# Two layers on one core: between the layers, weight splits are held back while the first token tile is normalised, and half of that tile's scaling moves from ScalarE to VectorE

## The chip, the cores and the metric

The kernel runs on one core of one Trainium2 chip. The metric is the device time of one execution in microseconds, and the lower the better. The kernel before was timed three times on the chip; a fourth execution was recorded by the hardware profiler, and all rows below are from that one.

## What is computed

Two transformer blocks of different kinds follow each other on 256 tokens of width 1024, in f32. What matters here is the passage from the first to the second:

```
# end of the first block
    return x + merged @ w_out[l]
...
    return _rmsnorm(x, final_norm_g)
...
# start of the second block
        h = rmsnorm(x, norm1_g[l]) * (1.0 + scale1) + shift1
        proj = h @ w_in[l]
        qa, ka, va, fa, qb, kb, vb, ga, gb = jnp.split(proj, IN_SPLITS, axis=-1)
```

So the output projection `merged @ w_out` and the residual are followed by two RMS norms in a row, a scale and a shift per column (they come from `c_2` through `ada_w_2`), and the input projection of the second block. After that block's attentions comes a mixture of 16 experts, whose weights are about 100 MB, and a last norm.

## The kernel before, in words

**Split matmuls.** A product of f32 matrices is made of three fast products: each operand is split into a high part (rounded to `fp32r`) and a low part (the rest), and low*high, high*low and high*high are summed in PSUM. Activations stand transposed in `H` (high) and `L` (low), eight blocks of 128 columns by 256 tokens. A weight unit is 1024 columns of a 128-row tile; it is split by one ScalarE copy (`self.sc.activation(h, raw, AF.Copy)` in `splitter`) and one VectorE subtraction (`split_low`), both 128x1024 between the layers. In the rows the tiles of split weights are called `w`, those of raw weights `ring`.

**Two token tiles.** The 256 tokens are two tiles of 128, `t` = 0 and 1 (first and second tile below). `out_proj` does `w_out` in eight parts for the first tile, then eight for the second. A part is one weight unit against one tile: six matmuls 128x512, two groups of three. The input projections that follow (`va` and `vb`, four weight units each, written by `job_a`) are woven by `weave` with `LAG2` = 5: five parts of the first tile, and then one of the first and one of the second in turn.

**The norm between the layers**, `mid_norm(t, banks)`, is a generator. On VectorE it adds the two PSUM banks to the residual (`X<-X,d`) and multiplies by a row (`tt<-X,ra`), for each half of the columns; ScalarE makes four sums of squares; VectorE adds them (`v<-ss`) and goes on with small steps; ScalarE takes a root (`s<-v`); five more small steps on VectorE, and then the scaled tile `xs<-tt,r` (128x1024). `affine_split` follows: TensorE transposes `xs` in two halves of four 128x128 blocks (`w<-cf,xs`), each half is multiplied by a column scale and a shift is added (`PP<-w`, four instructions), ScalarE rounds it (`H<-PP`), VectorE subtracts (`L<-PP,H`). Of the first tile both halves are scaled on ScalarE, of the second tile the first half on ScalarE and the second half on VectorE.

**What sets the order.** Instructions are written in the order that `Order`, a model of the engines' times inside the kernel's program, gives: generators are stepped when the modelled time reaches them. Every engine then works its own list in that order. `splitter` is one such generator; it splits the next weight unit as soon as its raw tile is there and a slot for the split tile is free, ahead of need. `self.v.` and `self.sc.` calls all show as L275, matmuls as L436, transposes as L452.

Of the kernel before, what the change touches and what calls it, by code (L numbers as in the profile page):

```python
# [97 lines left out]
class Pack:  # L98


    def __init__(self, x, ap):
        self.x, self.ap = x, ap
        self.parts = []
        self.where = {}
        self.at = 0
# [186 lines left out]
def wait(cond):  # L292
    while not cond():
        yield 0.1
# [27 lines left out]
class Body:  # L322
    def __init__(self, ctx, tc, a, pack):
        self.tc = tc
        self.pk = pack
        self.nc = nc = tc.nc
        self.a = a
        self.o = o = Order()
        self.v = Timed(o, "dve", nc.vector)
        self.sc = Timed(o, "act", nc.scalar)  # L330
        self.fix = ctx.enter_context(tc.tile_pool(name="fix", bufs=1))
        self.big = ctx.enter_context(tc.tile_pool(name="big", bufs=1))
        dram = ctx.enter_context(tc.tile_pool(name="dram", bufs=1, space=bass.MemoryType.DRAM))
        self.xd = dram.tile([2 * P, D], F32, name="xd")
        self.ps = ctx.enter_context(tc.tile_pool(name="ps", bufs=1, space=bass.MemoryType.PSUM))
        self.free = [f"ring{i}" for i in range(5)]
        self.slots = [f"spl{i}" for i in range(4)]
        self.until_unit = {}
        self.at = 0
        self.last_split = False  # L340
        self.pool = {k: [f"{k}{i}" for i in range(n)] for k, n in dict(d=4, w=4, p=4, th=3, sp=3).items()}
        self.held = {}
        self.turn = {}
        self.ada_first = Task(None)
        self.quiet = False
        self.t0_scaled = False
        self.chunks = []
        self.units = []
        self.items = []
        self.live = 0  # L350
        self.act_set = None
        self.exp_set = SET_EXP

# [140 lines left out]
    def splitter(self):  # L494

        for u in self.units:
            self.slots = [x for x in self.slots if self.until_unit.get(x, u.idx) >= u.idx]
            yield from wait(lambda: self.slots)
            u.tag = self.slots.pop(0)
            for c, view, lo, n, shape in u.srcs:  # L500
                while c.tile is None:
                    yield 0.1
                d = self.o.written(c.tile) - self.o.now
                if u.tile is None:
                    d = max(d, self.o.slot_end(u.tag) - self.o.now)
                if d > 0:
                    yield d
                if self.relaxed(u):
                    yield from self.yielding("act")
                if u.tile is None:  # L510
                    u.tile = self.slab(u.tag, "w")
                    u.h = u.tile[:, 0:1024].bitcast(F32R)
                    u.l = u.tile[:, 1024:2048].bitcast(F32R)
                raw = view(c.tile)
                h = u.h[:, lo:lo + n]
                l = u.l[:, lo:lo + n]
                if shape:
                    h = h.rearrange(shape[0], **shape[1])
                    l = l.rearrange(shape[0], **shape[1])
                self.sc.activation(h, raw, AF.Copy)  # L520
                self.o.spawn(self.split_low(u, c, raw, h, l), self.o.next - self.o.now)
                yield max(0.01, self.o.free["act"] - self.o.now - 0.3)
        self.last_split = True
        self.spare(self.slots)
        self.slots = []
# [257 lines left out]
    def affine_split(self, x, t, scale, marks, bias=None):  # L783

        def sink(k0, ps):
            eb = yield from self.take("p")
            e = eb.rearrange("p (j q) -> p j q", j=4)
            for j in range(4):
                k = k0 + j
                q = ps[:, j * P:(j + 1) * P]  # L790
                if (k0 == 0 or t == 0) and bias is not None:
                    self.act(e[:, j], q, AF.Identity, scale=scale[:, k:k + 1], bias=bias[:, k:k + 1])
                elif k0 == 0:
                    self.act(e[:, j], q, AF.Copy, scale=scale[:, k:k + 1])
                elif bias is not None:
                    self.v.tensor_scalar(e[:, j], q, scale[:, k:k + 1], bias[:, k:k + 1], OP.mult, OP.add)
                else:
                    self.v.tensor_scalar(e[:, j], q, scale[:, k:k + 1], None, OP.mult)
            if k0:
                yield  # L800
            h = self.xh[:, k0:k0 + 4, t * P:(t + 1) * P]
            self.act(h, e, AF.Copy)
            yield
            self.v.tensor_tensor(self.xl[:, k0:k0 + 4, t * P:(t + 1) * P], e, h.bitcast(F32), OP.subtract)
            self.drop(eb)
            yield
            marks[k0 // 4].fin = self.o.now
            marks[k0 // 4].done = True

        return self.transposed(x, sink)  # L810
# [384 lines left out]
    def mid_norm(self, t, banks):  # L1195

        v = self.v
        x = self.x[:, t]  # L1200
        ss = self.tmp("ss4", 2, 4)
        cs = [slice(b * 512, (b + 1) * 512) for b in range(2)]
        for b, c in enumerate(cs):
            if t == 1:
                yield from self.yielding("dve")
            v.tensor_tensor(x[:, c], x[:, c], banks[b], OP.add)
            self.drop(banks[b])
            v.tensor_tensor(self.tt[:, t, c], x[:, c], self.row_a[:, c], OP.mult)
        yield 0.7 if t == 0 else None
        for b, c in enumerate(cs):  # L1210
            self.act(self.xs[:, t, c], x[:, c], AF.Square, accum_out=ss[:, b:b + 1])
            self.act(self.xs[:, t, c], self.tt[:, t, c], AF.Square, accum_out=ss[:, 2 + b:3 + b])
        yield
        m = self.tmp("v2", 2, 2)
        s = self.tmp("s2", 2, 2)
        r = self.tmp("r2", 2, 4)
        v.tensor_tensor(m, ss[:, 0:4:2], ss[:, 1:4:2], OP.add)
        v.tensor_scalar(m[:, 0:1], m[:, 0:1], 1.0 / D, EPS, OP.mult, OP.add)
        v.tensor_scalar(s[:, 0:1], m[:, 0:1], EPS, None, OP.mult)
        v.tensor_scalar(m[:, 1:2], m[:, 1:2], 1.0 / D, s[:, 0:1], OP.mult, OP.add)  # L1220
        yield
        yield from self.root(r[:, 0:2], m, s)
        v.tensor_scalar(self.xs[:, t], self.tt[:, t], r[:, 1:2], None, OP.mult)
        yield

        yield from self.affine_split(self.xs[:, t], t, self.a1, self.n_marks[t], self.modc[:, 0])
        self.act(x, self.tt[:, t], AF.Copy, scale=r[:, 0:1])
# [949 lines left out]
```

## Time and profile before

| | |
|---|---|
| median of 3 runs | 714.19 us |
| lowest, highest | 713.5, 714.22 us |
| the profiled execution: time, span of its instructions | 714.5 us, 712.6 us |
| TensorE: busy time, share of the span | 688.1 us, 97% |
| VectorE, ScalarE: share of the span | 56%, 45% |
| DMA: mean rate over the span | 290 GB/s |
| mean granted TensorE clock | 0.984 |

The time of an execution is about 1.9 us longer than the span from its first to its last instruction. A time in a timeline row is counted from the span's start. In a timeline row "x8" is eight like instructions in a row, the second number is how long they took together, and what stands in brackets is how long the engine was idle before, and what it waited for.

### The profile page before, as it was taken

To read this page: it belongs to the slowest core of one execution; us is meant where nothing else is said; L and a number is where in the kernel's file an instruction comes from. 1 tells how busy PE (TensorE), PEld (TensorE's weight loads), DVE (VectorE), ACT (ScalarE), POOL (GpSimd) and SP (SyncE) were. 2 spreads that over 40 slices of the span, in tenths; PEclk is the share of its full clock that TensorE was granted. 3 is DMA by queue.
4 is the path that set the end of the run, shared out by engine and by line. 5 is a ranking of instruction groups with operands and counts; after the bars stand their busy time and mean duration, and the time that the engine had idled before them with its cause. 6 is when DMAs were issued, how large, how long until landed. Compare 5 with 4: busy or idle time off the path is not lost.

```text
span 712.6 us, 9923 instructions
## 1 busy us (share of the span) xinstructions
PE 688.1 (97%) x3860; PEld 492.9 (69%) x3862; DVE 397.5 (56%) x752; ACT 320.0 (45%) x613; POOL 9.1 (1%) x15
## 2 busy tenths in 40 slices
PE   7999999999999998999999999989999999999993
PEld 6999889878878886899877778876333433443431
DVE  6576687896756676686967846653211311321315
ACT  6544475564444667545668744522221121121113
POOL 0000000000000000000000000000000000000000
PEclk8999999999999999999999999999999999999997
DMA  9965657546756553555673895996999999999991
GB/s 354 381 231 220 267 186 282 184 177 236 288 184 245 181 224 119 214 229 204 241 295 137 329 361 183 351 385 268 417 422 420 420 423 420 420 421 418 421 364 63
DMA packets 31668, 206.35 MB, mean 290 GB/s; under 512 B 3968, under 2 KB 4480, under 8 KB 8448
## 3 DMA queue, kind: packets, MB, share of 16 engines
q1 hardware_dynamic: 29968, 200.82, 72.2%
q0 software_dynamic: 1072, 3.68, 1.3%
q10 hardware_dynamic: 576, 1.16, 0.4%
q8 instruction: 32, 0.52, 0.3%
q14 instruction: 20, 0.16, 0.1%
HBM read 203.55 MB, written 2.10 MB: 289 GB/s over the span
## 4 chain that ended last, share of the span: by engine, by line
PE 72%; DMA 21%; DVE 4%; ACT 1%; issue 1%; SPq 0%; DVEq 0%; ACTq 0%
PE d L436 53%; PE w L436 17%; DMA spl<-weights 6%; DMA L<-weights 6%; DMA YA<-weights 6%; DMA ring<-weights 3%; PE w L452 2%; DVE w L275 1%; DMA X<-x 1%; ACT xs L275 0%; DVE PP L275 0%; DVE L L275 0%; DVE X L1597 0%; ACT sq L275 0%; DVE sw L275 0%
## 5 line engine op out<-in xcount | busy, mean ns | idle before, releaser
L275 DVE TENSOR_TENSOR w<-ring,w 128x1024 fp32r<-128x1024 f32 (+1 forms) x166 | 156.6, 964 | 80.0 <-ACT w L275 79.7
L275 ACT ACTIVATE w<-ring 128x1024 fp32r<-128x1024 f32 (+1 forms) x166 | 136.1, 849 | 88.4 <-PE d L436 82.0
L436 PE MATMUL d<-w,H 128*128 128x512 f32 x448 | 141.1, 397 | 0.0
L436 PE MATMUL d<-H,w 128*128 128x256 f32 x672 | 121.8, 283 | 0.0
L436 PEld LDWEIGHTS d<-H,w 128*128 128x128 f32 x672 | 104.7, 192 | 0.1
L436 PEld LDWEIGHTS d<-w,H 128*128 128x128 f32 x448 | 85.9, 192 | 18.0 <-issue 0.5
L436 PE MATMUL d<-L,w 128*128 128x256 f32 x336 | 97.2, 289 | 0.0
L436 PE MATMUL d<-w,L 128*128 128x512 f32 x224 | 93.3, 416 | 3.8 <-DVE L L275 3.8
L436 PEld LDWEIGHTS d<-L,w 128*128 128x128 f32 x336 | 64.4, 192 | 1.2 <-issue 1.0
L1625 DVE TENSOR_TENSOR th<-th,w 128x512 f32<-128x512 f32 (+1 forms) x9 | 5.6, 628 | 102.2 <-PE w L436 102.2
L436 PE MATMUL d<-w,YA 128*128 128x512 f32 x224 | 60.6, 394 | 0.0
L275 ACT ACTIVATE th<-w 128x512 f32<-128x512 f32 (+1 forms) x16 | 9.3, 584 | 106.6 <-PE w L436 53.7
L436 PEld LDWEIGHTS d<-w,L 128*128 128x128 f32 x224 | 43.1, 192 | 14.7 <-DVE L L275 5.2
L275 DVE SCALAR_TENSOR_TENSOR acc<-ring,ca,acc 128x1024 f32<-128x1024 f32 x39 | 49.9, 1280 | 2.3 <-DMA ring<-weights 2.1
L436 PEld LDWEIGHTS d<-w,YA 128*128 128x128 f32 x224 | 41.9, 188 | 9.0 <-issue 0.3
L436 PE MATMUL w<-ring,ra 128*64 128x512 f32 x128 | 47.0, 598 | 0.0
L275 ACT ACTIVATE rg<-th 128x512 fp32r<-128x512 f32 x15 | 9.4, 630 | 55.0 <-DVE th L1652 34.8
L436 PE MATMUL w<-spl,ra 128*64 128x512 f32 x96 | 32.5, 596 | 0.0
L436 PEld LDWEIGHTS w<-ring,ra 128*64 128x64 f32 x128 | 13.5, 137 | 18.2 <-issue 17.7
L436 PE MATMUL w<-ring,th 128*64 128x512 f32 x72 | 25.5, 599 | 0.0
L275 ACT ACTIVATE PP<-w,sa 128x128 f32<-128x128 f32 (+1 forms) x48 | 19.7, 426 | 9.0 <-DVE sa L275 7.5
L436 PE MATMUL d<-w,YC 128*128 128x512 f32 x96 | 23.5, 399 | 0.0
(326 smaller groups left out, 1021.8 us busy)
## 6 DMA issues: line engine op xcount, KB each, us to landing
ring<-weights SPq DMA_DIRECT2D x109, 1024.0 KB, 6.4
spl<-weights SPq DMA_DIRECT2D x16, 1024.0 KB, 18.2
CQ<-weights SPq DMA_DIRECT2D x8, 1024.0 KB, 7.0
AB<-weights SPq DMA_DIRECT2D x6, 1024.0 KB, 14.3
K<-weights SPq DMA_DIRECT2D x6, 1024.0 KB, 13.5
PT<-weights SPq DMA_DIRECT2D x5, 1024.0 KB, 16.2
H<-weights SPq DMA_DIRECT2D x5, 1024.0 KB, 19.2
L<-weights SPq DMA_DIRECT2D x5, 1024.0 KB, 19.8
```

What stands on the lines that cost most here:

```text
L275: r = fn(*args, **kw)
L436: self.nc.tensor.matmul(out, lhsT, rhs, start=start, stop=stop)
L452: self.nc.tensor.transpose(out, in_, self.ident if ident is None else ident)
L1625: nc.vector.tensor_tensor(h[:, c], gate[:, c], res[1][:, c], OP.mult)
```

## The change

Three edits. First, a counter `budget` is put into `splitter`: None lets it split freely, 0 stops it, a positive number is counted down by one for each piece. `mid_norm` sets it to 0 when the first tile's norm begins and to 2 when the tile has been scaled (`xs`); `affine_split` sets it to 1 when the first half of the first tile has been split into `H` and `L`, and to None at the second half. Second, the first tile's second half is scaled on VectorE, as the second tile's is. Third, and by itself, the order in which `Order` steps everything around this place comes out anew.

```diff
@@ splitter
                 if self.relaxed(u):
                     yield from self.yielding("act")
+                yield from wait(lambda: self.budget != 0)
+                if self.budget:
+                    self.budget -= 1
                 if u.tile is None:
                     u.tile = self.slab(u.tag, "w")
...
@@ affine_split
-                if (k0 == 0 or t == 0) and bias is not None:
+                if k0 == 0 and bias is not None:
                     self.act(e[:, j], q, AF.Identity, scale=scale[:, k:k + 1], bias=bias[:, k:k + 1])
...
             self.drop(eb)
+            if bias is not None and t == 0:
+                self.budget = None if k0 else 1
             yield
...
@@ mid_norm
         x = self.x[:, t]
+        if t == 0:
+            self.budget = 0
         ss = self.tmp("ss4", 2, 4)
...
         v.tensor_scalar(self.xs[:, t], self.tt[:, t], r[:, 1:2], None, OP.mult)
+        if t == 0:
+            self.budget = 2
         yield
```

The lists of the engines differ only here, between the layers; before and behind it they read alike, and the DMA queues' lists are alike from end to end.

**VectorE, from the first tile's scaling to the second tile's sums.** Before, from `xs_2398<-tt,r_2433` of the first tile to `v_2551<-ss_2516` of the second (the other tiles are named above):

```order
L275 TENSOR_SCALAR xs_2398<-tt,r_2433 128x1024
L275 TENSOR_TENSOR w<-ring_2288,w 128x1024 x2
L275 TENSOR_TENSOR w<-ring_2328,w 128x1024 x2
L275 TENSOR_TENSOR L<-PP,H 128x4x128
L275 TENSOR_TENSOR X<-X,d_2400 128x512
L275 TENSOR_TENSOR tt<-X,ra 128x512
L275 TENSOR_TENSOR X<-X,d_2401 128x512
L275 TENSOR_TENSOR tt<-X,ra 128x512
L275 TENSOR_TENSOR w<-ring_2364,w 128x1024
L275 TENSOR_TENSOR L<-PP,H 128x4x128
L275 TENSOR_TENSOR v_2551<-ss_2516 128x2
```

Of the change, the same stretch:

```order
L275 TENSOR_SCALAR xs_2398<-tt,r_2431 128x1024
L275 TENSOR_TENSOR w<-ring_2245,w 128x1024 x2
L275 TENSOR_SCALAR PP<-w_2474,a_1548,modc 128x128 x4
L275 TENSOR_TENSOR L<-PP,H 128x4x128 x2
L275 TENSOR_TENSOR X<-X,d_2400 128x512
L275 TENSOR_TENSOR tt<-X,ra 128x512
L275 TENSOR_TENSOR w<-ring_2288,w 128x1024 x2
L275 TENSOR_TENSOR w<-ring_2328,w 128x1024 x2
L275 TENSOR_TENSOR w<-ring_2364,w 128x1024
L275 TENSOR_TENSOR X<-X,d_2401 128x512
L275 TENSOR_TENSOR tt<-X,ra 128x512
L275 TENSOR_TENSOR v_2572<-ss_2504 128x2
```

The pair of `ring_2245`, which stood ahead of the first tile's root, is now behind its scaling; the first tile's two `L` have moved ahead of four of the splits; and five splits now stand between the two halves of the second tile's residual (`d_2400` and `d_2401`), where none stood.

**TensorE, around the second tile's transposes.** Before (`w_2474` and `w_2485` are the two units of one raw tile of `vb`, `d3` is the first tile's sum, `w_2423` the first unit of `va`, and `d0_2608` the second tile's first sum):

```order
L436 MATMUL d3_2572<-w_2474,L_2397 128x512
L436 MATMUL d3_2572<-w_2474,H_2396 128x512 x2
L452 MATMUL w0_2580<-cf_72,xs2_2398 128x128 x4
L452 MATMUL w1_2585<-cf_72,xs2_2398 128x128 x4
L436 MATMUL d3_2572<-w_2485,L_2397 128x512
L436 MATMUL d3_2572<-w_2485,H_2396 128x512 x2
L436 MATMUL d3_2572<-w_2485,L_2397 128x512
L436 MATMUL d3_2572<-w_2485,H_2396 128x512 x2
L436 MATMUL d0_2608<-w_2423,L_2397 128x512
```

Of the change (`w_2528` and `w_2536` are those two units of `vb`, `w_2449` is the first of `va`):

```order
L437 MATMUL d3_2552<-w_2528,L_2397 128x512
L437 MATMUL d3_2552<-w_2528,H_2396 128x512 x2
L437 MATMUL d3_2552<-w_2536,L_2397 128x512
L437 MATMUL d3_2552<-w_2536,H_2396 128x512 x2
L437 MATMUL d3_2552<-w_2536,L_2397 128x512
L437 MATMUL d3_2552<-w_2536,H_2396 128x512 x2
L453 MATMUL w0_2586<-cf_72,xs2_2398 128x128 x4
L453 MATMUL w1_2591<-cf_72,xs2_2398 128x128 x4
L437 MATMUL d0_2608<-w_2449,L_2397 128x512
```

The transposes stand one part later: behind six of the first tile's parts instead of five, and the second tile's first matmul, which reads what comes of them, follows them at once.

**TensorE, around the first tile's transposes.** Before (`w_2361` and `w_2385` are the last two units of `w_out`, here against the second tile; `d2_2520` is the first sum of the second layer):

```order
L436 MATMUL d1_2401<-w_2361,YA_2073 128x512
L452 MATMUL w3_2488<-cf_72,xs2_2398 128x128 x4
L452 MATMUL w2_2496<-cf_72,xs2_2398 128x128 x4
L436 MATMUL d0_2400<-w_2385,CV_2074 128x512
L436 MATMUL d1_2401<-w_2385,CV_2074 128x512
```

Of the change:

```order
L437 MATMUL d1_2401<-w_2352,YA_2073 128x512
L453 MATMUL w3_2466<-cf_72,xs2_2398 128x128 x4
L453 MATMUL w2_2474<-cf_72,xs2_2398 128x128 x4
L437 MATMUL d0_2400<-w_2361,CV_2074 128x512
L437 MATMUL d1_2401<-w_2361,CV_2074 128x512
```

Here the transposes stand one part earlier: two parts of `w_out` are behind them instead of one.

## Rows read from the trace of the kernel before

**Rows 1.** The page: the span, and busy time of each engine.

```profile
span 712.6 us, 9923 instructions
PE 688.1 (97%) x3860; PEld 492.9 (69%) x3862; DVE 397.5 (56%) x752; ACT 320.0 (45%) x613; POOL 9.1 (1%) x15
```

**Rows 2.** Waits of TensorE by what ended them: total us, times, longest.

```profile
PE d L436 <- DVE L L275: 3.8, 3, 1.8
```

**Rows 3.** Timeline of TensorE between the layers: start, us.

```profile
263.63 0.62 PE L436 MATMUL d<-w,CV 128*128 128x512 f32 x2
...
265.00 1.03 PE L452 MATMUL w<-cf,xs 128*128 128x128 f32 x8
...
269.24 0.50 PE L436 MATMUL d<-w,L 128*128 128x512 f32 x1 [1.83 <-DVE L L275]
...
273.68 0.43 PE L436 MATMUL d<-w,L 128*128 128x512 f32 x1
...
277.86 1.04 PE L452 MATMUL w<-cf,xs 128*128 128x128 f32 x8
...
281.44 0.51 PE L436 MATMUL d<-w,L 128*128 128x512 f32 x1 [1.16 <-DVE L L275]
```

**Rows 4.** Windows: length, busy us by engine; PEclk, DMA share, GB/s.

```profile
10.00:14.00 4.00, 2.76 (x10) 2.27 (x11) 4.00 (x11) 3.94 (x12) 0.00 (x0) 0.55 1.02 412
268.00:272.00 4.00, 2.76 (x8) 2.20 (x9) 3.93 (x7) 3.97 (x11) 0.00 (x0) 0.72 0.96 395
...
280.00:284.00 4.00, 2.84 (x13) 2.14 (x12) 1.59 (x3) 3.05 (x4) 0.00 (x0) 1.00 0.00 0
```

**Rows 5.** Timeline of VectorE between the layers.

```profile
256.77 0.68 DVE L275 TENSOR_TENSOR X<-X,d 128x512 f32<-128x512 f32 x1
...
259.07 0.16 DVE L275 TENSOR_TENSOR v<-ss 128x2 f32<-128x2 f32 x1 [0.89 <-ACT xs L275]
...
260.02 2.36 DVE L275 TENSOR_TENSOR w<-ring,w 128x1024 fp32r<-128x1024 f32 x2 [0.16 <-ACT w L275]
...
263.29 0.75 DVE L275 TENSOR_SCALAR xs<-tt,r 128x1024 f32<-128x1024 f32 x1
263.95 4.63 DVE L275 TENSOR_TENSOR w<-ring,w 128x1024 fp32r<-128x1024 f32 x4
...
270.42 0.68 DVE L275 TENSOR_TENSOR X<-X,d 128x512 f32<-128x512 f32 x1
...
271.74 1.22 DVE L275 TENSOR_TENSOR w<-ring,w 128x1024 fp32r<-128x1024 f32 x1
...
273.48 0.15 DVE L275 TENSOR_TENSOR v<-ss 128x2 f32<-128x2 f32 x1
...
275.55 0.76 DVE L275 TENSOR_SCALAR xs<-tt,r 128x1024 f32<-128x1024 f32 x1
278.93 1.37 DVE L275 TENSOR_SCALAR PP<-w,a,modc 128x128 f32<-128x128 f32 x4 [2.63 <-PE w L452]
280.69 1.29 DVE L275 TENSOR_TENSOR L<-PP,H 128x512 fp32r<-128x512 f32 x2 [0.39 <-ACT H L275]
```

**Rows 6.** Timeline of ScalarE between the layers.

```profile
260.94 3.95 ACT L275 ACTIVATE w<-ring 128x1024 fp32r<-128x1024 f32 x4
...
278.50 1.50 ACT L275 ACTIVATE PP<-w,modc,a 128x128 f32<-128x128 f32 x4 [1.21 <-PE w L452]
280.03 1.15 ACT L275 ACTIVATE H<-PP 128x512 fp32r<-128x512 f32 x2
```

**Rows 7.** Timeline of TensorE at the kernel's start: the first block's transposes.

```profile
10.44 1.97 PE L452 MATMUL w<-cf,xs 128*128 128x128 f32 x8 [0.96 <-DVE xs L275]
```

**Rows 8.** Windows of the second layer, its end, and the experts (columns as in Rows 4).

```profile
300.00:472.00 172.00, 171.84 (x1049) 144.21 (x1049) 116.21 (x184) 97.67 (x181) 0.78 (x1) 1.00 0.70 264
488.00:492.00 4.00, 3.94 (x20) 1.23 (x18) 3.37 (x22) 1.39 (x2) 0.00 (x0) 1.00 0.02 6
500.00:530.00 30.00, 29.12 (x140) 10.53 (x136) 5.78 (x15) 6.30 (x11) 0.98 (x1) 1.00 1.01 420
```

More of the change, by code (lines that the diff above doesn't have):

```diff
@@ L350, in __init__ @@
         self.live = 0
+        self.budget = None
         self.act_set = None
```

## The prediction

> **What bounds the kernel now.** I read the page's busy times first: TensorE is busy for 688.1 us of a span of 712.6 [rows 1], so what can be won or lost in the middle is idle TensorE, or TensorE at its lower clock. The list of its waits comes next: matmuls that waited for `L` of VectorE lost 3.8 us in three places [rows 2]. One lies in the first block's beginning; the timeline of TensorE shows the other two, and both are between the layers [rows 3]: 1.83 us at 269.24, where the first tile's first input projection waits for the normalised tile, and 1.16 us at 281.44, where the second tile's does. The first has a sequel. The granted clock over 268 to 272 is 0.72, a mixture of full speed and half (the levels are 2.4 and 1.2 GHz), while behind the shorter second stall it stays at 1.00 [rows 4]. The four groups from 269.24 to 273.68 are two parts [rows 3]; a part at full clock is the 1.37 us from the matmul at 263.63 to the transposes at 265.00, so 4.44 us were spent on 2.74 us of work, 1.70 us lost. All that this place has to give is therefore 1.83 + 1.16 + 1.70 = 4.7 us.
>
> A delay or a gain here reaches the end. From 300 to 472 TensorE is busy for 171.84 of 172 us, so nothing in the second layer takes it up. At 488 to 492 the DMA share is 0.02: the transfers have filled every buffer and wait for TensorE to free one; from 500 on they run at a share of 1.01 [rows 8]. The experts' stream thus starts when TensorE gets there, and is moved with it.
>
> **The first tile, step by step.** *The root earlier.* The pair of splits that filled VectorE from 260.02 for 2.36 us, while the root was wanted, is moved behind the scaling. The second tile of before shows the way from the sums to the scaling with no split between: 273.48 to 275.55, 2.07 us [rows 5]. From 259.07 that gives 261.14 for the scaling and, with its 0.75 us, 261.9 for its end, where before it ended at 264.04. The counter costs no instruction.
>
> *Transposes.* They stand one part earlier, so at 263.63 instead of 265.00 [rows 3], with `xs` ready for 1.7 us by then.
>
> *Half of the scaling on VectorE.* Four take 1.37 us there and 1.50 on ScalarE, and the halves go side by side [rows 5, 6]. The second tile of before is made just so: from its transposes at 277.86 to `L` at 280.69 are 2.83 us, to the first matmul at 281.44 are 3.58 [rows 3, 5]. VectorE is free for it: 261.9 + 2.36 = 264.3, wanted at 263.63 + 1.07 = 264.7. So the first matmul may start at 263.63 + 3.58 = 267.2.
>
> *The stall.* TensorE still has two parts of `w_out` behind the transposes: 263.63 + 1.03 + 2 x 1.37 = 267.4, the same as before (265.00 + 1.03 + 1.37). The wait of 1.83 us is gone, and with it the 1.70 us of low clock. Were this all, TensorE would be 3.5 us ahead.
>
> **The second tile.** *Where VectorE is late.* Behind the first tile's two `L` (266.46, and 1.29 us for both) comes the first half of the second tile's residual with its product: 1.32 us, as from 270.42 to 271.74 [rows 5]. That is 269.07. Then five splits stand ahead of the second half. Four took 4.63 us [rows 5], so five take 5.79. ScalarE doesn't hold them: it ends `H` at 263.63 + (280.03 + 1.15 - 277.86) = 266.95 and has six steps of 128x1024 (five splits and a copy of `X`) at 3.95 / 4 = 0.99 us [rows 6], so it is through at 272.9, and VectorE begins its fifth at 273.7. The second half of the residual starts at 269.07 + 5.79 = 274.86, and before at 270.42.
>
> From there to the sums are 2.30 us if ScalarE waits for nothing else (first tile, 256.77 to 259.07), to the scaling 2.07, and the scaling takes 0.76 [rows 5]: 279.99. The second tile's transposes stood at 277.86 and start at 280.0, so 2.13 us later.
>
> *Where TensorE now waits.* From 267.4 it works off six parts, to 267.4 + 6 x 1.37 = 275.6, and then has 4.4 us of idle in front of the transposes. Before, 1.37 us of matmuls stood behind the transposes, and hid part of the way to `L`; now that part is ahead of them, and the way of 3.58 us is idle but for the transposes. The next matmul starts at 280.0 + 3.58 = 283.6 against 281.44: **+2.13 us**, with all that was won at the first tile lost in idle.
>
> *The clock.* An idle of 1.83 us had the clock at half in the next matmuls, one of 1.16 had not [rows 3, 4]. This place was not seen with 4.4 us of idle and more behind it, so the price is bounded: nothing, if the clock stays, and at most what half speed costs. I take the row it resembles, the longer stall. Transposes at half speed took 1.97 us at the kernel's start, where the clock of 10 to 14 is 0.55, against 1.03 at full [rows 3, 4, 7]. ScalarE needs the first four of them; half of the difference is **+0.47 us**, so that the next matmul starts at 284.1. Then **+1.70 us** for the first parts, as at 269.24; the same loss of before lies ahead of 281.44, and is in that number already.
>
> On this the Trainium skill, "TensorE: Matmul & The Clock Gate", section "What's actually happening", says that the array's normal state is the throttled one, that activity lifts it, and that the loss at the start differs from run to run. By that page the sum could come out with the two clock terms or without, which is 4.3 or 2.1 us; the trace agrees as far as two idles of like length had unlike sequels.
>
> *The rest.* Raw tiles are released later, the pair of `ring_2288` by some 5 us (its splits end at 271.4 instead of about 266); what is loaded into them next serves the query projection, which comes behind the sixteen parts of `va` and `vb`, some 22 us of TensorE. The four scalings taken from ScalarE free 1.50 us at a place where it is not waited for.
>
> **Sum.** 2.13 + 0.47 + 1.70 = 4.3 us. The profiled execution took 714.5 us for a span of 712.6, 0.3 above the median of 714.19; 712.6 becomes 716.9, and the median **718.5 us**. A measurement of this kernel can tell about 0.2%, 1.4 us, from no change.
>
> **The rivals.**
>
> *No clock loss* (0.12). The clock stays at full speed at the transposes and behind them: +2.1, 716.3 us. For it: the 1.16 us stall without a sequel. Against it: the idle is more than twice that which had one.
>
> *A longer loss* (0.09). Transposes alone don't lift the clock, the idle behind them keeps it down, and the way to the first parts at half speed is longer than at 269.24; twice the 1.70 gives 720.2 us.
>
> *Faster* (0.08). The second half of the residual doesn't stand behind all the splits in time, because ScalarE or TensorE is elsewhere than I reckon. If it followed the first half at once, at 269.07, the second tile would be ready at 274.2, ahead of the 275.6 at which TensorE comes; the next matmul would start at 275.6 + 3.58 = 279.2, which is 2.2 us ahead of before: 712.0 us. The point that decides is that start: without a clock loss the change is even when it lies at 272.7, so with three splits ahead of it; with the loss at 270.6, with one. Against it: VectorE works its list in order, and five stand there.
>
> *Absorbed* (0.05). The shift is taken up behind the layers, and the time stays at 714.2. For it only that TensorE's busy share hides waits inside its matmuls; against it the 171.84 of 172 us, and the empty DMA queue at 488.
>
> **Chances and range.** 718.5 has 0.66, and by itself reaches from 717.4 to 719.6 (the clock terms half as large, or half as large again). The range, 715.6 to 720.6, takes in the rivals on its sides but leaves out the two in which nothing is lost, 0.13. Slower by over 0.2%: 0.66 + 0.12 + 0.09 = 0.87; within: 0.05; faster: 0.08.
>
> **What would show it.** In the profile of the changed kernel: the first tile's scaling at about 261.1 and its transposes at 263.6; no stall of TensorE near 267.4; the second half of the residual at 274.9; transposes of the second tile at 280 behind an idle of 4 us that ends with `xs`, and an idle of 2 to 3 us that ends with `L`; the next matmul near 284, and a clock well under 1 in the window from 284 to 288. I am wrong if TensorE comes to the second tile's transposes and finds `xs` ready, or if the clock in that window is 1.

## The result and the profile after

| | before | change |
|---|---|---|
| median | 714.19 us | 720.17 us |
| lowest, highest (5 runs each) | 713.39, 715.15 us | 717.65, 720.38 us |
| the profiled execution: time, span | 714.5, 712.6 us | 720.17, 718.3 us |

The change is slower: the ratio of its time to that of before is 1.0069, with an interval of 1.0053 to 1.0085, so 4.9 us (3.8 to 6.1). The two medians lie further apart, 6.0 us: two of the change's five runs took 717.65 and 717.89 us and three 720.17 to 720.38, and the median is one of the three. What follows goes by the ratio. A second series of the change gave a median of 719.86 us and 1.0064 (1.0048 to 1.008).

The page of the change, the lines that answer to [rows 1]:

```profile
span 718.3 us, 9924 instructions
PE 690.0 (96%) x3862; PEld 493.4 (69%) x3862; DVE 399.1 (56%) x756; ACT 319.0 (44%) x609; POOL 9.1 (1%) x15
```

The span has grown by 5.7 us and TensorE's busy time by 1.9 (its matmuls at half clock count as busy). The rest is idle, and the list of TensorE's waits (total us, times, longest) says for what; to be held against [rows 2]:

```profile
PE w L453 <- DVE xs L275: 5.1, 2, 4.1
PE d L437 <- DVE L L275: 3.8, 2, 2.1
```

The wait for `L` has the total that it had, but not between the layers. One of its two pieces lies in the first block's beginning, where both kernels read alike and where it was 0.80 us before (3.8 - 1.83 - 1.16):

```profile
13.18 0.80 PE L437 MATMUL d<-w,L 128*128 128x512 f32 x1 [1.67 <-DVE L L275]
```

Between the layers it has fallen from 1.83 + 1.16 = 2.99 us in two places to 2.13 in one. New is the wait of the transposes for `xs`, 4.1 us of it in one place. The timeline of TensorE between the layers shows that place:

```profile
263.28 1.03 PE L453 MATMUL w<-cf,xs 128*128 128x128 f32 x8
...
266.88 0.48 PE L437 MATMUL d<-w,L 128*128 128x512 f32 x1
...
269.71 0.39 PE L437 MATMUL d<-w,L 128*128 128x512 f32 x1
...
279.53 1.94 PE L453 MATMUL w<-cf,xs 128*128 128x128 f32 x8 [4.09 <-DVE xs L275]
283.60 0.79 PE L437 MATMUL d<-w,L 128*128 128x512 f32 x1 [2.13 <-DVE L L275]
...
289.89 0.39 PE L437 MATMUL d<-w,L 128*128 128x512 f32 x1
```

The first tile's transposes are followed by its first matmul at 266.88 with no wait ([rows 3]: 1.83 us), and the row at 269.71 is the fifth group of three matmuls, which started at 273.68 before. The second tile's transposes come behind 4.09 us of idle, and 2.13 us more stand ahead of its first matmul. From 283.60 to 289.89 are five groups of three matmuls, 6.29 us; at full clock a group takes half of a part's 1.37 us, so 5 x 0.684 = 3.42, and 2.87 us were lost there.

VectorE's timeline, to be held against [rows 5]:

```profile
260.77 0.75 DVE L275 TENSOR_SCALAR xs<-tt,r 128x1024 f32<-128x1024 f32 x1
...
267.32 0.68 DVE L275 TENSOR_TENSOR X<-X,d 128x512 f32<-128x512 f32 x1
...
268.65 5.76 DVE L275 TENSOR_TENSOR w<-ring,w 128x1024 fp32r<-128x1024 f32 x5
274.32 0.68 DVE L275 TENSOR_TENSOR X<-X,d 128x512 f32<-128x512 f32 x1
...
276.58 0.16 DVE L275 TENSOR_TENSOR v<-ss 128x2 f32<-128x2 f32 x1 [0.85 <-ACT xs L275]
...
278.63 0.75 DVE L275 TENSOR_SCALAR xs<-tt,r 128x1024 f32<-128x1024 f32 x1
```

The five splits between the two halves of the second tile's residual take 5.76 us in one piece, and all that the transposes wait for is behind them. The windows (columns as in [rows 4]) show the clock, and that nothing later takes the delay up:

```profile
276.00:280.00 4.00, 0.47 (x3) 0.50 (x4) 2.25 (x10) 0.75 (x3) 0.00 (x0) 0.92 0.39 162
280.00:284.00 4.00, 1.87 (x8) 1.47 (x7) 2.46 (x6) 3.22 (x7) 0.00 (x0) 0.50 0.01 4
284.00:288.00 4.00, 4.00 (x10) 3.06 (x10) 0.61 (x2) 1.63 (x2) 0.00 (x0) 0.50 0.00 0
288.00:292.00 4.00, 4.00 (x16) 3.24 (x15) 1.43 (x2) 1.16 (x2) 0.00 (x0) 0.80 0.47 166
...
300.00:476.00 176.00, 176.00 (x1088) 147.68 (x1085) 120.62 (x189) 99.14 (x184) 0.78 (x1) 1.00 0.70 269
```

A granted clock of 0.50 is 1.2 GHz: the transposes, 1.94 us against 1.04 before, and the groups behind them ran at that level.

**A ruler.** A span also holds what differs between executions elsewhere, so the profiles are compared between two fixed instructions of TensorE: from the part of `w_out` ahead of which the change puts the first tile's transposes (263.63 before [rows 3], 263.28 in the change) to the transposes of `X` for the router at the second layer's end; and from there to the experts' first matmuls. The timeline of TensorE, before:

```profile
472.29 0.60 PE L452 MATMUL w<-cf,X 128*128 128x128 f32 x4
...
488.28 3.65 PE L436 MATMUL w<-ring,ra 128*64 128x512 f32 x16
```

And in the change:

```profile
477.14 0.60 PE L453 MATMUL w<-cf,X 128*128 128x128 f32 x4
...
494.50 3.65 PE L437 MATMUL w<-ring,ra 128*64 128x512 f32 x16
```

The passage grew from 472.29 - 263.63 = 208.66 to 477.14 - 263.28 = 213.86, by 5.20 us. The stage behind it took 15.99 and 17.36 us, another 1.37; that this is not the change's doing shows below.

### The profile page after: what moved, and what is told of

Read it like the earlier page. It is cut to its first block, busy times and chain, and to the rows that moved or that the text cites. A ratio compares the mean times of both kernels' runs of the same rounds, so it can differ in the third digit from the quotient of the medians.

```text
span 718.3 us, 9924 instructions
## 1 busy us (share of the span) xinstructions
PE 690.0 (96%) x3862; PEld 493.4 (69%) x3862; DVE 399.1 (56%) x756; ACT 319.0 (44%) x609; POOL 9.1 (1%) x15
## 3 DMA queue, kind: packets, MB, share of 16 engines
q0 software_dynamic: 1072, 3.68, 1.3%
q10 hardware_dynamic: 576, 1.16, 0.4%
## 4 chain that ended last, share of the span: by engine, by line
PE 78%; DMA 15%; DVE 4%; ACT 1%; issue 1%; SPq 0%; DVEq 0%; ACTq 0%
PE d L437 54%; PE w L437 21%; DMA spl<-weights 6%; PE w L453 3%; DMA ring<-weights 3%; DMA YA<-weights 3%; DMA L<-weights 3%; DVE w L275 1%; DMA X<-x 1%; DVE PP L275 1%; ACT xs L275 0%; DVE L L275 0%; DVE X L275 0%; DVE X L1607 0%; ACT sq L275 0%
```

## The experiments

Eight runs, of seven other kernels and of the change once more, each timed beside the kernel before on the same chip. All of them on the ruler (us; the passage is the difference of the two starts, and its change is against 208.66; the experts' column counts from the router's transposes):

| kernel | from | to | passage | change | to experts | ratio of times (interval) |
|---|---|---|---|---|---|---|
| before | 263.63 | 472.29 | 208.66 | | 15.99 | 1 |
| the change | 263.28 | 477.14 | 213.86 | +5.20 | 17.36 | 1.0069 (1.0053, 1.0085) |
| the change again | 263.36 | 476.41 | 213.05 | +4.39 | 15.99 | 1.0064 (1.0048, 1.008) |
| halves together | 263.32 | 476.08 | 212.76 | +4.10 | 17.37 | 1.0033 (1.002, 1.0047) |
| idle filled | 264.54 | 475.30 | 210.76 | +2.10 | 15.98 | 1.0038 (1.0024, 1.0053) |
| scaling alone | 263.81 | 476.39 | 212.58 | +3.92 | 15.98 | 1.0063 (1.0046, 1.008) |
| counter alone | 263.23 | 474.63 | 211.40 | +2.74 | 15.98 | 1.005 (1.0031, 1.007) |
| second tile first | 263.16 | 471.30 | 208.14 | -0.52 | 17.61 | 0.9975 (0.9962, 0.9988) |
| the same, filled | 263.14 | 471.35 | 208.21 | -0.45 | 15.99 | 0.9986 (0.9974, 0.9999) |
| before, filled | 263.44 | 472.05 | 208.61 | -0.05 | 17.31 | 0.9994 (0.9983, 1.0005) |

The last stage has two lengths, about 16.0 and 17.3 to 17.6 us, and the change itself shows both: it goes by the execution, not by the kernel. What differs in it is the clock. From the router's transposes to its second eight matmuls of `w<-rwa,PP` both executions of the change take 4.05 us; those eight and the 28 rows of unused matmuls of ones behind them (`self.warm(14)`) then take 1.90 and 5.57 us in the long one, 1.07 and 5.00 in the short one. The granted clock from 480 to 484 and from 484 to 488 is 0.59 and 0.56 in the long one, 0.79 and 0.78 in the short one.

**The second tile's residual in one piece.** VectorE yields to other work ahead of the first half only, so that both halves stand together:

```diff
         for b, c in enumerate(cs):
-            if t == 1:
+            if t == 1 and b == 0:
                 yield from self.yielding("dve")
```

> The change, with the second tile's two residual halves next to each other on VectorE (no step aside between them). Theory A (the five splits ahead of the second half make the second tile late): the second half starts near 268.7 instead of 274.3; three splits and two more still stand in the small steps behind it, so the scaled tile comes only about 1 us earlier (transposes near 278.6 instead of 279.5, idle before them about 3.2 instead of 4.1 us), and the time falls by about 1 us, or by up to 2.5 if the clock recovers earlier: 717.5 to 719 against 720.2. Theory B (the held-back splits or the VectorE scaling of the first tile cost the time, not this order): no change, 720.2. Theory C (the place in the list alone counts, nothing behind it): the 5.6 us by which the second half moves all come back, about 714.6.

Measured: 717.1 us, ratio 1.0033. VectorE's timeline:

```profile
268.69 0.68 DVE L275 TENSOR_TENSOR X<-X,d 128x512 f32<-128x512 f32 x1
...
270.01 3.49 DVE L275 TENSOR_TENSOR w<-ring,w 128x1024 fp32r<-128x1024 f32 x3
...
274.25 1.23 DVE L275 TENSOR_TENSOR w<-ring,w 128x1024 fp32r<-128x1024 f32 x1
275.71 1.23 DVE L275 TENSOR_TENSOR w<-ring,w 128x1024 fp32r<-128x1024 f32 x1 [0.24 <-ACT w L275]
...
277.84 0.75 DVE L275 TENSOR_SCALAR xs<-tt,r 128x1024 f32<-128x1024 f32 x1
```

And TensorE's:

```profile
278.74 1.07 PE L453 MATMUL w<-cf,xs 128*128 128x128 f32 x8 [1.78 <-DVE xs L275]
282.35 0.79 PE L437 MATMUL d<-w,L 128*128 128x512 f32 x1 [2.54 <-DVE L L275]
```

The second half starts 5.6 us sooner and the transposes only 0.8, as the same five splits now stand behind it: three ahead of the sums and two among the small steps. So it is not the place of one instruction that makes the second tile late, but that five splits lie anywhere in its chain on VectorE. By the ratios 2.6 us of the loss are gone, the upper end of what theory A allowed; on the ruler 1.1. The profiled execution, at 719.1 us, was one of the longer of its twelve; it ran five groups behind 282.35 at half clock, as the change's did, and had the longer router stage.

**The idle filled.** The change, with 18 matmuls of ones ahead of the second tile's transposes and 10 behind them (each shows as two in the rows). Their results are not used.

```diff
+    def fill(self, n):
+        ps = self.take_now("d")
+        for _ in range(n):
+            self.nc.tensor.matmul(ps[:, :P], self.ones, self.ones, start=True, stop=True)
+        self.drop(ps)
...
+        if t == 1:
+            self.fill(18)
+            self.gap = 10
         yield from self.affine_split(self.xs[:, t], t, self.a1, self.n_marks[t], self.modc[:, 0])
```

> The change, with 18 matmuls of ones (128x128) ahead of the second tile's transposes and 10 behind them, in TensorE's idle; the lists are otherwise the same, and the matmuls' results are used by nothing. Theory A (half of the loss is the clock): the granted clock stays at 1.00 from 276 to 290, the transposes take 1.03 us instead of 1.94, the next matmul starts near 283.1 instead of 283.6, and the five groups behind it take 3.4 us instead of 6.3: about 3.3 us less, near 716.9. Theory C (only the wait counts, and the lower clock is hidden or made up later): within 0.5 us of 720.2.

Measured: 717.68 us, ratio 1.0038. TensorE's timeline and one of the windows:

```profile
276.52 4.18 PE L457 MATMUL d<-ones 128*128 128x128 f32 x36
280.79 1.06 PE L461 MATMUL w<-cf,xs 128*128 128x128 f32 x8
281.69 2.40 PE L457 MATMUL d<-ones 128*128 128x128 f32 x20
...
284.49 0.47 PE L438 MATMUL d<-w,L 128*128 128x512 f32 x1 [0.41 <-DVE L L275]
```

```profile
284.00:288.00 4.00, 3.59 (x16) 2.93 (x16) 1.70 (x3) 2.24 (x3) 0.00 (x0) 1.00 0.00 0
```

The next matmul comes 19.95 us behind the first tile's transposes (20.32 in the change), so it is 0.37 us sooner, for transposes at full speed; the wait is otherwise as long as it was, but the clock stays at 1.00. This separates the two causes. The wait alone costs 2.1 us on the ruler, which is the 19.95 - 17.81 by which the next matmul is later than before (281.44 - 263.63 = 17.81), and 2.7 by the ratio. The clock is the rest: by the ratios 1.0069 - 1.0038, some 2.2 us, though their intervals just touch; on the ruler 3.1 against the first profile of the change and 2.3 against the second. The Trainium skill, "TensorE: Matmul & The Clock Gate", section "What's actually happening", says that activity is what lifts the throttle; this window, at 1.00 where the change had 0.50, agrees.

**Each edit by itself.** The first is before with the moved scaling only; the second is the change with the first tile's second half left on ScalarE.

```diff
# scaling alone, in the kernel before
-                if (k0 == 0 or t == 0) and bias is not None:
+                if k0 == 0 and bias is not None:
# counter alone, in the change
-                if k0 == 0 and bias is not None:
+                if (k0 == 0 or t == 0) and bias is not None:
```

> The kernel before with only the first tile's second half scaled on VectorE; splits are not held. Theory A: the scaling stands behind four splits on VectorE, the first L comes at about 269.9 instead of 268.5, the first stall grows from 1.8 to about 3.2 us; the second tile's transposes are again behind six parts and the next matmul is at about 284 instead of 281.4: 2 to 3 us slower than before, about 716.5. Theory B (the VectorE scaling itself is what costs, and holding the splits pays): slower than the change, over 720. If the scaling paid for itself alone: under 713.

> The change with the first tile's second half scaled on ScalarE as before; splits are held. Theory A: the first tile's first matmul still starts near 267.2, then several short stalls (the second L about 1.7 us late, and 0.5 to 1 us at each of the two last units), the second tile's transposes near 279 and the next matmul near 282.6 to 283: 1 to 2 us slower than before at full clock, up to 3 with a clock loss: 715 to 717. Theory B (holding the splits is what costs): 720 or more.

Measured: 718.59 us, ratio 1.0063, and 718.32 us, ratio 1.005. TensorE's timeline with the scaling alone:

```profile
270.69 0.80 PE L436 MATMUL d<-w,L 128*128 128x512 f32 x1 [3.11 <-DVE L L275]
...
280.44 1.07 PE L452 MATMUL w<-cf,xs 128*128 128x128 f32 x8
284.05 0.79 PE L436 MATMUL d<-w,L 128*128 128x512 f32 x1 [2.55 <-DVE L L275]
...
287.73 0.39 PE L436 MATMUL d<-w,L 128*128 128x512 f32 x1
```

With the counter alone:

```profile
271.34 0.50 PE L437 MATMUL d<-w,L 128*128 128x512 f32 x1 [1.52 <-DVE L L275]
...
278.57 1.07 PE L453 MATMUL w<-cf,xs 128*128 128x128 f32 x8 [0.33 <-DVE xs L275]
282.18 0.51 PE L437 MATMUL d<-w,L 128*128 128x512 f32 x1 [2.54 <-DVE L L275]
...
286.62 0.39 PE L437 MATMUL d<-w,L 128*128 128x512 f32 x1
```

Neither edit pays by itself, and each keeps the first tile's wait in some form: the scaling alone makes it longer, since VectorE's scaling and `L` queue behind the splits that are still there. Common to both and to the change is the second tile: its next matmul stands directly behind its transposes, and waits 2.1 to 2.6 us for `L`. With either edit alone it comes 3.61 us behind their start (3.58 before), so what counts is when they start. With the counter alone that is 1.1 us later than before, counted from the ruler's first mark, and they still wait 0.33 for `xs`. With the scaling alone it is 2.4 later, and they wait for nothing: TensorE itself comes there late, behind the longer first wait and one part more. Both runs lost more time than expected: the scaling 3.9 us on the ruler for 2 to 3, the counter 2.7 (3.6 by the ratio) for 1 to 2, or up to 3 with a clock loss. The next matmuls came where they were expected, at 284.05 and 282.18; what came on top is the half clock behind them, three groups in 3.68 us and four in 4.44, so 1.6 and 1.7 us lost, at a granted clock of 0.50 from 284 to 286 in both.

**The second tile first.** If the splits in the second tile's chain are the cause, holding most of them back there too must pay. The halves stand together as above, and the counter is set to 2 behind either tile's scaling, to 1 behind each half of the first tile, and to None only at the second tile's second half:

```diff
-            if bias is not None and t == 0:
-                self.budget = None if k0 else 1
+            if bias is not None:
+                self.budget = 1 if t == 0 else None if k0 else self.budget
...
-        if t == 0:
-            self.budget = 2
+        self.budget = 2
```

> The change with the second tile's norm kept free as well: its two residual halves next to each other, two units split while it runs (one behind each half of the first tile), two more when it is scaled, all others only behind its second L. Theory A (what the change loses, it loses by splits that stand on VectorE ahead of the second tile's norm): the second tile's transposes at about 275.3 instead of 279.5, two of the first tile's parts behind them, the next matmul at about 279.7 (before 281.4, the change 283.6), idle in three pieces of 0.5 to 1.6 us; the time 4 to 6 us under the change, 1 to 2 under the kernel before, or level with it if the short idles cost the clock. Theory B (holding splits starves TensorE of weights): no better than the change.

Measured: 713.56 us (712.47 to 715.25, 11 runs), ratio 0.9975. TensorE's timeline:

```profile
271.13 0.73 PE L437 MATMUL d<-w,H 128*128 128x512 f32 x2 [1.12 <-DVE w L275]
...
275.15 1.06 PE L453 MATMUL w<-cf,xs 128*128 128x128 f32 x8 [1.23 <-DVE xs L275]
...
276.81 0.74 PE L437 MATMUL d<-w,H 128*128 128x512 f32 x2 [0.36 <-DVE w L275]
...
279.83 0.50 PE L437 MATMUL d<-w,L 128*128 128x512 f32 x1 [0.23 <-DVE L L275]
...
282.10 0.73 PE L437 MATMUL d<-w,H 128*128 128x512 f32 x2 [0.39 <-DVE w L275]
```

VectorE's row of the second tile's scaling, and two of the windows:

```profile
274.25 0.75 DVE L275 TENSOR_SCALAR xs<-tt,r 128x1024 f32<-128x1024 f32 x1
```

```profile
272.00:276.00 4.00, 2.77 (x18) 2.14 (x16) 2.92 (x12) 2.41 (x6) 0.00 (x0) 1.00 0.69 229
...
280.00:284.00 4.00, 3.61 (x15) 2.66 (x16) 2.98 (x3) 2.78 (x3) 0.00 (x0) 1.00 0.52 213
```

Two splits are left in the second tile's chain instead of five. Counted from the first tile's transposes, its scaling starts at 15.35 us in the change (278.63 - 263.28), at 14.52 with the halves together (277.84 - 263.32) and at 11.09 here (274.25 - 263.16). Putting the halves together thus brings 0.83 us, and the three splits fewer bring 3.43; three splits took 3.49. Its transposes come 11.99 us behind the first tile's (275.15 - 263.16) instead of 16.25, first-tile matmuls stand behind them again and hide the way to `L`, and the idle is in short pieces, at a clock of 1.00. This version beats both kernels, before by 1.8 us by the ratio (0.9 to 2.7). The ruler shows 0.52 us of that, though the profiled execution was the longest of the eleven; where the rest lies is not settled.

**Its idle filled.** The same with 6 matmuls of ones ahead of the second tile's transposes, `self.fill(6)`, to see whether a clock loss is left there:

> As the kernel that keeps the second tile's norm free, with six matmuls of ones ahead of the second tile's transposes (results unused), in an idle of 1.6 us. Theory A: no stretch at half clock between the layers, 2 to 3.5 us under the kernel before, and under the unfilled one by up to 1.7 us if that one loses the clock, level with it if not. Theory C: level with the unfilled one.

Measured: 714.3 us, ratio 0.9986, with the transposes at 275.13. There was no loss left to win back; the intervals of the two versions overlap, and over before this one gains 1.0 us (0.1 to 1.9).

**Before, with its longer stall filled.** The kernel before, with 8 matmuls of ones ahead of the first input projection, `self.item(None, lambda: self.fill(8))`. It asks whether the half clock behind that stall costs anything.

> The kernel before with eight matmuls of ones (128x128, results unused) in the first stall, ahead of the second layer's first matmul; nothing else differs. Theory A (the stall's sequel, 1.70 us at half clock, is in the time): the clock stays at 1.00 from 268 to 276, the stall itself stays as long, and the time falls by about 1.7 us. Theory C (the lower clock is hidden or made up later): within 0.5 us of the kernel before.

Measured: 715.02 us, ratio 0.9994 (0.9983 to 1.0005). TensorE's timeline:

```profile
267.06 1.95 PE L455 MATMUL d<-ones 128*128 128x128 f32 x16
269.14 0.47 PE L436 MATMUL d<-w,L 128*128 128x512 f32 x1
...
273.44 0.50 PE L436 MATMUL d<-w,L 128*128 128x512 f32 x1 [1.32 <-DVE L L275]
```

The clock stayed at 1.00 from 264 to 292, and the four groups from 269.14 were done sooner; then TensorE waited 1.32 us for the second half of the first tile's `L`. The fifth group starts at 273.44, and in [rows 3] at 273.68 with all four at a mixed clock: the same but for 0.05 us, since this execution was 0.19 ahead. The half clock of before filled a wait that was there anyway. The expected gain of 1.7 us did not come.

**The change again**, unaltered, for its clock:

> The change itself once more, beside the other runs and on the same chip. Theory A: 4 to 6 us over the kernel before, the next matmul 2 to 2.5 us later than in it, and the rest in stretches at half clock, whose length differs from one execution to the next.

Measured: 719.86 us, ratio 1.0064. TensorE's timeline:

```profile
279.62 1.94 PE L453 MATMUL w<-cf,xs 128*128 128x128 f32 x8 [4.10 <-DVE xs L275]
283.69 0.79 PE L437 MATMUL d<-w,L 128*128 128x512 f32 x1 [2.13 <-DVE L L275]
...
287.69 0.43 PE L437 MATMUL d<-w,L 128*128 128x512 f32 x1
```

Waits and starts repeat to 0.1 us. The half clock does not: three groups from 283.69 to 287.69, 4.00 us for 3 x 0.684 = 2.05 of work, so about 2.0 us lost, where the first profile lost 2.87.

## Why the prediction was right, and where it was off

*The first tile: right.* Scaling at 260.77 (261.14 predicted; all of this execution is 0.35 ahead), transposes at 263.28, and no stall at 266.88.

*The second tile late by the five splits: right.* Counted from the ruler's first mark, the second half of the residual was predicted at 274.86 - 263.63 = 11.23 and came at 274.32 - 263.28 = 11.04; the transposes at 16.37 and 16.25; the idle ahead of them 4.4 and 4.09. That these splits are the cause is shown by the versions with five and with two of them behind two halves that stand together: three fewer, and the scaling 3.43 us earlier.

*The next matmul directly behind the transposes: right.* Predicted 20.47 behind the mark (284.1 - 263.63), measured 20.32, against 281.44 - 263.63 = 17.81 before: +2.51 for a predicted 2.13 + 0.47. The transposes took 1.94 us, as priced from [rows 7].

*The clock behind it: right in kind, the size in part luck.* The term "+1.70 us for the first parts, as at 269.24" was taken from the longer stall of before. It measured 2.87 and 2.0 us in two profiles. Both clock terms together, 0.47 + 1.70 = 2.17, came out at 2.2 by the ratio of the filled idle, but at 3.1 and 2.3 on the ruler. The stretch that lent the 1.70 cost nothing where it lay (before, filled), and its length is that of one execution; that it came so near is luck. The rival without a clock loss falls (0.50 from 280 to 288). That of a longer loss, at twice 1.70 = 3.4, was too much, but of the 2.87 in the first profile it was the nearer, and in kind it held: the transposes didn't lift the clock, and the idle behind them left it at half. The Trainium skill, "TensorE: Matmul & The Clock Gate", section "What's actually happening", says of the start of a kernel that the loss differs from run to run. In the middle of this one it did too: 2.87 and 2.0 us behind the same idle.

*To the end: right.* TensorE was busy for all 176.00 us from 300 to 476. The sum of 4.3 lies within the 3.8 to 6.1 measured. The median, 720.17, is in the range but above the 717.4 to 719.6 that 718.5 was given by itself, and on the 720.2 of the longer loss. It is no proof of that rival: the execution that is the median is the profiled one, and it holds the longer router stage. That the profiled execution was longer by 5.7 is for 1.37 us the stage of the router, which has two lengths whatever the kernel; the prediction had no term for it.

*What failed.* "All that this place has to give is therefore 1.83 + 1.16 + 1.70 = 4.7 us" put 1.70 us on the clock, which by itself gives nothing back: before, filled, runs at 0.9994, since the second half of the first tile's `L` was not there sooner. The 3.5 us by which TensorE "would be ahead" did come, for another reason: its fifth group starts 10.05 us behind the mark before (273.68 - 263.63) and 6.43 in the change (269.71 - 263.28), 3.62 sooner, because both halves of `L` were there and not because the clock was up. Neither figure is in the sum, since the second tile's norm sets the time behind it. The rival "faster" was wrong in its point too: with the second half of the residual at 268.69, well ahead of its 272.7, the kernel was still slower, as the splits moved to behind it. Between these versions the number of splits in the whole chain up to `xs` decides, not that start. It is not all that counts: with the scaling alone `xs` was not waited for, and the next matmul still came 2.4 us later than before.

*Left open.* Why the best version gains more by its ratio than its ruler shows (the first block and the router's stage, which differ from one execution to the next, lie outside the ruler, but no run tells how much of it they hold); and what decides how long the half clock lasts.

## What to carry to other kernels

Work that is held back from one chain stands somewhere else: follow it on its engine's list, and if another chain that the bound engine waits for is there, the gain is lost or worse. A stall or a half clock is worth something only if the engine has no later wait that would take it up; filling the idle with unused matmuls tests that, and whether the clock matters, in one run. To compare profiles whose difference is under one per cent, measure between two fixed instructions, and see what else differs between two executions of the same kernel.

## What the hardware did that was not expected

The same idle of 4.1 and 2.1 us was followed by five groups at half clock in one execution and by three in another. Idle of 1.12, 1.23, 0.36, 0.23 and 0.39 us with matmuls between them left the clock at 1.00, as did 1.52 us at 271.34 with the counter alone and 1.32 at 273.44 in before, filled, while a single 1.83 us in [rows 3] had half clock behind it in [rows 4]. The stage between the router's transposes and the experts took 15.98 or 15.99 us in six of the ten profiles and 17.31 to 17.61 in four, the change itself among both; between its two executions the whole difference lies in matmuls that ran at half clock for longer.
